# Two key units between the value tiles instead of ahead of them

## The chip, the cores and the metric

One core of a Trainium2 chip runs the whole program. The metric is the device time of one execution in microseconds (us), as the median of several runs. A profiled execution gives, beside its own time, the span from the first to the last instruction and the trace of every engine: TensorE (PE in the rows; PEld is its weight load), VectorE (DVE), ScalarE (ACT), GpSimd (POOL) and SyncE's queue of transfers (SPq). Every engine works through a queue of its own in the order in which the program gives it.

## What is computed

A decoder trunk of two layers over 1024 positions of width 1024. Only the first layer's mixer is touched: a native sparse attention beside a short gated convolution, both fed by one input projection.

```python
def even_mixer(h, w_in, cmp_pe, cmp_w1, cmp_w2, conv_w, w_out, cos, sin):
    z = h @ w_in
    q = apply_rope(z[..., :o1]...)                    # 8 heads of 64
    kv = z[..., o1:o2].reshape(bsz, s, 6, A_KV_HEADS, HEAD_DIM)
    gates = z[..., o2:o3]
    bc = z[..., o3:]                                  # short convolution
    kc = compress(apply_rope(kv[:, :, 0], cos, sin), cmp_pe[0], cmp_w1[0], cmp_w2[0])
    vc = compress(kv[:, :, 1], cmp_pe[1], cmp_w1[1], cmp_w2[1])
    ks = apply_rope(kv[:, :, 2], cos, sin)            # keys of the selected blocks
    kw = apply_rope(kv[:, :, 4], cos, sin)            # keys of the window
    o_a = nsa_attention(q, kc, vc, ks, kv[:, :, 3], kw, kv[:, :, 5], gates)
    ...
```

After it come the output projection, a gated convolution FFN, a recurrent layer and a second FFN; none of them is changed.

## The kernel before

Activations lie with features on the partitions and positions on the free axis. All products are made at near full precision from two halves: every operand is split into a rounded part (`wh`, `hh`) by a copy on ACT and a remainder (`wl`, `hl`) by a subtraction on DVE, and `mm3` (L144 to L148) issues three matmuls for each product, one of them with `wl` and one with `hl`.

The projection's columns come in pieces:

- A **unit** (`units`, L163) is 128 features by 1024 positions: 48 matmuls of 512 columns into one tile `U` of PSUM. The generator `gen` gives eight of them in the order compress keys, compress values, selected keys, window keys, four query units. The first two run together; `load_w` brings the weights of each later one (a 512 KB transfer into `wr`, then `wh` on ACT L132 and `wl` on DVE L133). `wr`, `wh` and `wl` have two buffers each.
- `c_unit` (L521) turns a compress unit into `xc`: rotation (`rope_unit`, for the keys), four copies into the staging tile `xf` on ACT (L532), and the split into `xc` (L151 on ACT, L152 on DVE). There is one `xf`: the second unit's copies wait until DVE has read the first one's.
- `k_unit` (L510) turns a key unit into `KH` and `KL`: four copies of 32 partitions on ACT (`rz`, L503 and L504), three full passes on DVE (`rz`, `rt`, L505 to L507), two copies to `KH` (L517) and two subtractions to `KL` (L518). It puts four duplicating copies on the list `dups`; they are issued on ACT after the value stage (L1034, L1035).
- A **value tile** (`v_proj`, L651) is 128 positions by 280 columns (four value heads' columns and 24 gates): 24 matmuls of 280 columns into a tile `V` of the same four PSUM buffers as `U`, then one copy on ACT and two operations on DVE (`VS` L667 and L668, `GS` L669). There are eight. Their weights `wvh`, `wvl` come in three pieces of 3, 3 and 2 chunks (`v_weights`, L640). After five tiles, and again after all eight, `cmp_mm` (L592) makes the compress hidden layer: 48 matmuls of 132 columns into `ub`, with two weight loads of 512 KB.

In `even_layer` the order written is: two compress units, key unit 0, weights of the value tiles, key unit 1, eight value tiles with the two `cmp_mm`, the duplicating copies, the query units. A scheduler places the instructions of each engine in a queue; it follows the written order, and may bring a later instruction forward where it takes an earlier one to be waiting. Once built, the queues are fixed.

Of the kernel before, what the change touches and what calls it, by code (L numbers as in the profile page):

```python
# [59 lines left out]
class Kern:  # L60
# [590 lines left out]
    def v_proj(self, H, wh, wl):  # L651
        nc, io = self.nc, self.io
        w1 = self.cmp_w(0)
        hvs = []
        for tt in range(8):
            if tt == self.vsplit:
                hvs.append(self.cmp_mm(0, w1))
                w1 = self.cmp_w(1)
            U = self.newU("V")
            ts = slice((tt % 4) * P, (tt % 4) * P + P)  # L660
            for kc in range(KC):
                hi, lo = H[kc][tt // 4]
                self.mm3(U[:, :280], hi[:, ts], lo[:, ts], wh[:, kc], wl[:, kc], kc == 0, kc == KC - 1)
            uv = U[:, :256].rearrange("p (b d) -> p b d", b=4)
            rc = self.rcol[:, tt:tt + 1]
            hi = self.VS[tt][:, :, :64]
            nc.scalar.activation(hi, uv, AF.Copy, scale=rc)  # L667
            nc.vector.scalar_tensor_tensor(self.VS[tt][:, :, 64:], uv, rc, hi.bitcast(FP), op0=OP.mult, op1=OP.subtract)  # L668
            nc.vector.tensor_scalar(self.GS[:, tt], U[:, 256:280], rc, None, op0=OP.mult)  # L669
        hvs.append(self.cmp_mm(1, w1))  # L670
        nc.scalar.activation(self.GS, self.GS, AF.Sigmoid)
        return hvs

    def select(self, i, imp):
        nc, tp = self.nc, self.tp
# [280 lines left out]
    def even_layer(self, fin):  # L956
# [9 lines left out]
        def opened(name, **kw):  # L966
            st = ExitStack()
            return st, st.enter_context(self.pool(name, **kw))
# [16 lines left out]
        H = nm["H"]  # L985
# [4 lines left out]
        with self.pool("xp", side="right") as xp, self.pool("np0", side="right") as self.np:  # L990
# [26 lines left out]
            gen = self.units(srcs, H, 2, mid, ws, 4)  # L1017
            U0 = next(gen)
        with self.pool("xc", side="right") as xc:
            self.XC = [[xc.tile([P, 2, 8, 68], FR, name=f"xc{a}{b}") for b in range(2)] for a in range(2)]  # L1020
            with self.pool("xf", side="right") as xf:
                self.xf = xf.tile([P, 2, 8, 68], FP, name="xf")
                nc.vector.memset(self.xf[:, :, :, 64:], 0.0)
                self.c_unit(0, U0)
                self.c_unit(1, next(gen))
            vs, vp = opened("VS")
            self.VS = [vp.tile([P, 4, P], FR, name=f"VS{t}") for t in range(8)]
            with self.pool("wv") as wp:
                Us, self.dups = [next(gen)], []
                wv = self.v_weights(wp)  # L1030
                self.k_unit(0, Us[0])
                self.k_unit(1, next(gen))
                hvs = self.v_proj(H, *wv)
            for o, t in self.dups:  # L1034
                nc.scalar.activation(o, t, AF.Copy)  # L1035
            box = self.compress1(cp, hvs)
# [734 lines left out]
```

## Time and profile before

| | |
|---|---|
| median of 3 runs | 2360.34 us (2357.21 to 2365.05) |
| profiled execution, own time | 2362.92 us |
| its span, first to last instruction | 2361.0 us |
| PE busy in the span | 2271.9 us (96%) |
| DVE, ACT, POOL busy | 1672.5 us (71%), 1162.0 us (49%), 137.3 us (6%) |

The shares are means over stages that have different limits. The change lies between about 37 and 104 us of the span, so the rows further down are read from there: which engine has a gap, and which instruction of which other engine ended last before the gap closed. A row of the timeline has the start and the length in us, the engine, the line, the operation, what it writes and reads, how many instructions the row merges and, in brackets, how long the engine stood idle before it and what ended that.

### The profile page before, as it was taken

The numbers are of one execution on the slowest core, as the hardware profiler recorded it, in microseconds if no ns is written. First come the engines' busy times: TensorE is split into PE (matmuls) and PEld (weight loads), VectorE is DVE, ScalarE is ACT, GpSimd is POOL, SyncE is SP. The second block draws the span as 40 slices with busy tenths as digits, with TensorE's granted clock in tenths as the row PEclk, the third lists the DMA queues.
The fourth block names the chain that finished last, engine by engine and source line by source line (L and its number), as shares of the span: only waits on it lengthen the run. The fifth ranks groups of instructions, "written<-read, shape, count | busy, mean of one in ns | idle before, by whom it ended". The sixth has DMA issues, their size and how long they took to land.

```text
span 2361.0 us, 26600 instructions
## 1 busy us (share of the span) xinstructions
PE 2271.9 (96%) x10190; PEld 1830.7 (78%) x10190; DVE 1672.5 (71%) x2459; ACT 1162.0 (49%) x1718; POOL 137.3 (6%) x102
## 2 busy tenths in 40 slices
PE   8999998999989999999999999999899999999998
PEld 6877776777667888887888777887678888878876
DVE  5566878988798777777434766768987777773446
ACT  7653666666645444444111474575554444441114
POOL 0002233311000000000000300000000000000000
PEclk9999999999999999999999999999999999999999
DMA  4223112222512222216222101113122222162222
GB/s 145 77 74 107 42 54 83 79 81 86 205 52 76 84 84 84 84 65 232 99 78 74 59 30 63 45 47 116 54 90 81 81 81 81 63 242 88 81 77 76
DMA packets 70464, 206.24 MB, mean 87 GB/s; under 512 B 7873, under 2 KB 11457, under 8 KB 70209
## 3 DMA queue, kind: packets, MB, share of 16 engines
q1 hardware_dynamic: 65376, 194.83, 24.1%
q10 hardware_dynamic: 4320, 7.61, 0.9%
q8 instruction: 80, 1.31, 0.2%
q0 software_dynamic: 640, 2.10, 0.2%
q14 instruction: 48, 0.39, 0.1%
HBM read 162.57 MB, written 41.94 MB: 87 GB/s over the span
## 4 chain that ended last, share of the span: by engine, by line
PE 72%; DVE 10%; ACT 5%; issue 2%; DMA 1%; POOL 0%; DVEq 0%; ACTq 0%; POOLq 0%
PE q L146 11%; PE q L148 11%; PE q L147 11%; PE D L148 7%; PE D L146 7%; PE D L147 7%; PE U L147 2%; PE U L146 2%; PE U L148 2%; PE T L842 2%; PE O L825 2%; PE F L146 1%; PE F L147 1%; PE F L148 1%; DVE P L817 1%
## 5 line engine op out<-in xcount | busy, mean ns | idle before, releaser
L132 ACT ACTIVATE wh<-wr 128x1024 fp32r<-128x1024 f32 x112 | 118.5, 1059 | 375.2 <-PE D L147 282.9
L1250 ACT ACTIVATE z<-q 128x512 f32<-128x512 f32 x176 | 103.7, 593 | 363.0 <-PE q L148 358.0
L264 DVE TENSOR_TENSOR x<-D,x 128x512 f32<-128x512 f32 x192 | 124.1, 686 | 216.2 <-PE D L148 216.1
L258 DVE SCALAR_TENSOR_TENSOR o<-z,par,o 128x1023 f32<-128x1023 f32 (+1 forms) x176 | 225.6, 1282 | 27.9 <-ACT o L256 24.9
L146 PE MATMUL q<-h,sh 128*128 128x512 f32 x480 | 190.3, 396 | 3.6 <-ACT z L1250 3.6
L148 PE MATMUL q<-h,sl 128*128 128x512 f32 x480 | 189.2, 394 | 0.0
L147 PE MATMUL q<-h,sh 128*128 128x512 f32 x480 | 188.7, 393 | 0.0
L146 PE MATMUL D<-y,wh 128*128 128x512 f32 (+1 forms) x464 | 181.1, 392 | 0.3 <-ACT y L151 0.3
L148 PE MATMUL D<-y,wl 128*128 128x512 f32 (+1 forms) x464 | 180.8, 390 | 0.0
L147 PE MATMUL D<-y,wh 128*128 128x512 f32 (+1 forms) x464 | 180.8, 390 | 0.0
L146 PE MATMUL U<-hh,wh 128*128 128x512 f32 x400 | 159.5, 399 | 12.1 <-ACT wh L132 12.1
L147 PE MATMUL U<-hl,wh 128*128 128x512 f32 x400 | 158.9, 398 | 0.0
L148 PE MATMUL U<-hh,wl 128*128 128x512 f32 x400 | 158.4, 397 | 0.0
L146 PE MATMUL q<-h,wh 128*128 128x512 f32 x320 | 126.5, 395 | 4.1 <-ACT wh L151 4.1
L133 DVE TENSOR_TENSOR wl<-wr,wh 128x1024 fp32r<-128x1024 f32 x88 | 111.5, 1266 | 26.6 <-ACT wh L132 23.3
L148 PE MATMUL q<-h,wl 128*128 128x512 f32 x320 | 127.6, 399 | 0.6 <-DVE wl L152 0.5
L147 PE MATMUL q<-h,wh 128*128 128x512 f32 x320 | 126.9, 397 | 0.0
L802 ACT ACTIVATE P<-P,m 128x640 f32<-128x640 f32 (+7 forms) x128 | 93.5, 731 | 46.9 <-DVE m L800 46.4
L256 ACT ACTIVATE o<-z,par 128x1024 f32<-128x1024 f32 x88 | 108.6, 1234 | 7.1 <-DMA fd<-o 4.5
L152 DVE TENSOR_TENSOR pl<-T,ph 128x512 fp32r<-128x512 f32 x132 | 89.3, 686 | 30.9 <-ACT ph L151 27.9
L1253 DVE TENSOR_TENSOR z<-q,z 128x512 f32<-128x512 f32 x132 | 90.1, 687 | 28.7 <-PE q L148 28.7
L146 PEld LDWEIGHTS q<-h,sh 128*128 128x128 f32 x480 | 90.4, 188 | 25.5 <-ACT z L1250 4.5
(362 smaller groups left out, 5777.8 us busy)
## 6 DMA issues: line engine op xcount, KB each, us to landing
wv<-in_wup SPq DMA_DIRECT2D x44, 512.0 KB, 5.4
wr<-in_wup SPq DMA_DIRECT2D x44, 512.0 KB, 4.7
fd<-o SPq DMA_DIRECT2D x44, 512.0 KB, 3.0
wr<-in_wd SPq DMA_DIRECT2D x40, 512.0 KB, 3.7
yr<-fd SPq DMA_DIRECT2D x36, 512.0 KB, 4.3
wr<-in_wbc SPq DMA_DIRECT2D x24, 512.0 KB, 3.5
wr<-in_cin SPq DMA_DIRECT2D x16, 512.0 KB, 3.6
yd<-y SPq DMA_DIRECT2D x24, 256.0 KB, 2.0
```

Of the source, the lines that this page charges most:

```text
L132: nc.scalar.activation(hi[:, s], raw[:, s], AF.Copy)
L133: eng.tensor_tensor(lo[:, s], raw[:, s], hi[:, s].bitcast(FP), op=OP.subtract)
L146: mm(out, whi, xhi, start=first, stop=False, skip_group_check=resumed)
L147: mm(out, whi, xlo, start=False, stop=False, skip_group_check=resumed)
L148: mm(out, wlo, xhi, start=False, stop=last, skip_group_check=resumed)
L152: (eng or self.nc.vector).tensor_tensor(lo, t, hi.bitcast(FP), op=OP.subtract)
L256: nc.scalar.activation(o, src, AF.Identity, bias=b, scale=w(K - 1))
L258: nc.vector.scalar_tensor_tensor(o[:, s:], src[:, :n - s], w(K - 1 - s), o[:, s:], op0=OP.mult, op1=OP.add)
L264: nc.vector.tensor_tensor(x, ps, x, op=OP.add)
L802: nc.scalar.activation(p, p, AF.Exp, bias=m, scale=-1.0, accum_out=s)
L1250: self.nc.scalar.activation(out, x, AF.Copy)
L1253: self.nc.vector.tensor_tensor(out, a, b, op=op)
```

## The change

`v_proj` becomes a generator that stops after each value tile and gives the compress results last. `even_layer` loads the value weights first, then makes three value tiles, key unit 0, three value tiles, key unit 1, and the last two.

```diff
--- before.py
+++ after.py
@@ -667,9 +667,10 @@
             nc.scalar.activation(hi, uv, AF.Copy, scale=rc)
             nc.vector.scalar_tensor_tensor(self.VS[tt][:, :, 64:], uv, rc, hi.bitcast(FP), op0=OP.mult, op1=OP.subtract)
             nc.vector.tensor_scalar(self.GS[:, tt], U[:, 256:280], rc, None, op0=OP.mult)
+            yield None
         hvs.append(self.cmp_mm(1, w1))
         nc.scalar.activation(self.GS, self.GS, AF.Sigmoid)
-        return hvs
+        yield hvs
@@ -1025,12 +1026,18 @@
             self.VS = [vp.tile([P, 4, P], FR, name=f"VS{t}") for t in range(8)]
-            with self.pool("wv") as wp:
-                Us, self.dups = [next(gen)], []
-                wv = self.v_weights(wp)
-                self.k_unit(0, Us[0])
-                self.k_unit(1, next(gen))
-                hvs = self.v_proj(H, *wv)
+            wst, wp = opened("wv")
+            wv = self.v_weights(wp)
+            self.dups = []
+            vgen = self.v_proj(H, *wv)
+            for br, tt in ((0, 3), (1, 3)):
+                for _ in range(tt):
+                    next(vgen)
+                self.k_unit(br, next(gen))
+            hvs = []
+            for hv in vgen:
+                hvs = hv
+            wst.close()
             for o, t in self.dups:
                 nc.scalar.activation(o, t, AF.Copy)
```

The number of instructions on each engine stays the same, and from the first query unit on the queues of before and after are equal. Up to there they differ. Three places follow; the number behind a tile's name tells tiles of one kind apart.

TensorE where the first two (compress) units end, before: `U_297` is the second compress unit, `U_474` key unit 0.

```order
L147 MATMUL U_297<-hl_290,wh_206 128x512
L148 MATMUL U_297<-hh_289,wl_207 128x512
L146 MATMUL U_474<-hh_185,wh_392 128x512
L147 MATMUL U_474<-hl_186,wh_392 128x512
L148 MATMUL U_474<-hh_185,wl_393 128x512
```

The same place after: `V_500`, `V_528` and `V_556` are the first three value tiles, `U_584` is key unit 0, with the same weights `wh_392`.

```order
L147 MATMUL U_297<-hl_290,wh_206 128x512
L148 MATMUL U_297<-hh_289,wl_207 128x512
L146 MATMUL V_500<-wvh,hh_185 128x280
L146 MATMUL V_528<-wvh,hh_185 128x280
L146 MATMUL V_556<-wvh,hh_185 128x280
L146 MATMUL U_584<-hh_185,wh_392 128x512
L147 MATMUL V_500<-wvl,hh_185 128x280
```

The value tiles' first matmuls, which need `wvh`, now stand directly behind the compress units; one matmul of key unit 0 is between them, the other 47 stand behind the three tiles.

ScalarE at the same place, before: `rz_543` belongs to key unit 0, `xf` and `xc` to the compress units, `wvh` are the value weights.

```order
L132 ACTIVATE wh_525<-wr_523 128x1024
L532 ACTIVATE xf<-rt_411 64x8x64 x4
L151 ACTIVATE xc_401<-xf 128x1088
L503 ACTIVATE rz_543<-U_474 32x1024
L504 ACTIVATE rz_543<-U_474 32x1024
L532 ACTIVATE xf<-rt_450 64x8x64 x4
L503 ACTIVATE rz_543<-U_474 32x1024
L151 ACTIVATE xc_403<-xf 128x1088
L504 ACTIVATE rz_543<-U_474 32x1024
L151 ACTIVATE wvh<-wr_531 128x840
```

After:

```order
L532 ACTIVATE xf<-rt_411 64x8x64 x4
L151 ACTIVATE xc_401<-xf 128x1088
L532 ACTIVATE xf<-rt_450 64x8x64 x4
L151 ACTIVATE xc_403<-xf 128x1088
L151 ACTIVATE wvh<-wr_476 128x840
L151 ACTIVATE wvh<-wr_480 128x840
L151 ACTIVATE wvh<-wr_484 128x560
```

The weights of key unit 1 and the copies of key unit 0 are gone from this stretch; `wvh` still stands behind both compress units' `xf` and `xc`.

ScalarE ahead of the first query unit, before: `wh_1027` are that unit's weights, `VS` and `GS` the value tiles' results.

```order
L667 ACTIVATE VS_469<-V_859,rcol 128x4x64
L667 ACTIVATE VS_470<-V_887,rcol 128x4x64
L671 ACT_TABLE_LOAD
L671 ACTIVATE GS<-GS 128x192
L132 ACTIVATE wh_1027<-wr_1025 128x1024
```

After, from the weights of the second `cmp_mm` on (`wh_765`); `U_797` is key unit 1.

```order
L132 ACTIVATE wh_765<-wr_763 128x1024
L503 ACTIVATE rz_846<-U_797 32x1024
L504 ACTIVATE rz_846<-U_797 32x1024
L503 ACTIVATE rz_846<-U_797 32x1024
L504 ACTIVATE rz_846<-U_797 32x1024
L667 ACTIVATE VS_469<-V_859,rcol 128x4x64
L667 ACTIVATE VS_470<-V_887,rcol 128x4x64
L517 ACTIVATE KH_126<-rt_847 64x1024
L517 ACTIVATE KH_127<-rt_847 64x1024
L672 ACT_TABLE_LOAD
L672 ACTIVATE GS<-GS 128x192
```

and directly behind these:

```order
L1042 ACTIVATE KH_126<-rt_847 64x1024
L1042 ACTIVATE KL_130<-KL_130 64x1024
L1042 ACTIVATE KH_127<-rt_847 64x1024
L1042 ACTIVATE KL_131<-KL_131 64x1024
L132 ACTIVATE wh_1027<-wr_1025 128x1024
```

The whole work on key unit 1, its four duplicating copies included, now stands between the second `cmp_mm`'s weights and those of the first query unit.

## Rows read from the trace of the kernel before

**Rows 1.** Windows: length; busy us (instructions) of PE, PEld, DVE, ACT, POOL; PEclk; DMA.

```profile
37.50:60.00 22.50, 22.50 (x97) 17.89 (x95) 9.09 (x9) 18.61 (x19) 0.00 (x0) 1.00 0.10 34
60.00:84.30 24.30, 19.38 (x123) 18.90 (x123) 19.11 (x24) 22.31 (x25) 0.00 (x0) 0.86 0.30 99
84.30:104.20 19.90, 19.90 (x169) 19.90 (x169) 6.84 (x14) 8.72 (x13) 0.00 (x0) 1.00 0.18 54
104.20:160.00 55.80, 55.32 (x241) 44.60 (x240) 30.39 (x36) 32.85 (x40) 0.00 (x0) 1.00 0.20 59
```

**Rows 2.** Timeline of PE, key units, value tiles and both compress products.

```profile
53.38 0.39 PE L148 MATMUL U<-hh,wl 128*128 128x512 f32 x1
...
59.69 0.39 PE L148 MATMUL U<-hh,wl 128*128 128x512 f32 x1
60.79 0.40 PE L146 MATMUL V<-wvh,hh 128*128 128x280 f32 x1 [0.71 <-ACT wvh L151]
62.21 0.50 PE L147 MATMUL V<-wvl,hh 128*128 128x280 f32 x1 [1.03 <-DVE wvl L152]
...
79.43 0.57 PE L146 MATMUL V<-wvh,hh 128*128 128x280 f32 x1 [3.18 <-DVE GS L669]
...
84.13 0.23 PE L146 MATMUL ub<-xc,wh 128*128 128x132 f32 x1
...
89.44 0.34 PE L146 MATMUL V<-wvh,hh 128*128 128x280 f32 x1
...
98.75 0.23 PE L146 MATMUL ub<-xc,wh 128*128 128x132 f32 x1
...
104.06 0.44 PE L146 MATMUL U<-hh,wh 128*128 128x512 f32 x1
```

**Rows 3.** Timeline of ACT, from the second compress unit's copies to the value weights.

```profile
52.21 4.37 ACT L532 ACTIVATE xf<-rt 64x512 f32<-64x512 f32 x4
...
57.65 1.11 ACT L151 ACTIVATE xc<-xf 128x1088 fp32r<-128x1088 f32 x1
...
59.83 1.70 ACT L151 ACTIVATE wvh<-wr 128x840 fp32r<-128x840 f32 x2
...
65.09 0.67 ACT L151 ACTIVATE wvh<-wr 128x560 fp32r<-128x560 f32 x1 [1.50 <-DMA wr<-in_wv]
```

**Rows 4.** Timeline of DVE and the transfer queue in the same stretch.

```profile
50.27 1.29 DVE L152 TENSOR_TENSOR xc<-xf,xc 128x1088 fp32r<-128x1088 f32 x1 [4.50 <-ACT xc L151]
...
61.13 1.97 DVE L152 TENSOR_TENSOR wvl<-wr,wvh 128x840 fp32r<-128x840 f32 x2
...
62.18 0.33 SPq L647 DMA_DIRECT2D wr<-in_wv  x1
...
65.80 0.74 DVE L152 TENSOR_TENSOR wvl<-wr,wvh 128x560 fp32r<-128x560 f32 x1 [0.30 <-ACT wvh L151]
```

**Rows 5.** Groups, 35 to 130 us: count | busy us, mean ns | idle before, releaser.

```profile
L133 DVE TENSOR_TENSOR wl<-wr,wh 128x1024 fp32r<-128x1024 f32 x10 | 12.2, 1224 | 15.7 <-ACT wh L132 15.7
L132 ACT ACTIVATE wh<-wr 128x1024 fp32r<-128x1024 f32 x9 | 9.4, 1058 | 13.8 <-PE U L147 8.0 <-PE ub L147 5.7
L504 ACT ACTIVATE rz<-U 32x1024 f32<-32x1024 f32 x9 | 9.2, 1019 | 0.1
L505 DVE TENSOR_TENSOR rt<-U,rope 128x1024 f32<-128x1024 f32 x4 | 4.9, 1223 | 5.5 <-ACT rz L504 5.5
L1035 ACT ACTIVATE KH<-rt 64x1024 fp32r<-64x1024 f32 x4 | 4.2, 1056 | 0.1
L517 ACT ACTIVATE KH<-rt 64x1024 fp32r<-64x1024 f32 x4 | 4.2, 1053 | 0.1
L668 DVE SCALAR_TENSOR_TENSOR VS<-V,rcol,VS 128x256 fp32r<-128x256 f32 x8 | 3.8, 481 | 8.9 <-ACT VS L667 8.8
L671 ACT ACT_TABLE_LOAD x1 | 1.3, 1283 | 0.0
L671 ACT ACTIVATE GS<-GS 128x192 f32<-128x192 f32 x1 | 0.4, 364 | 0.0
```

## Prediction, made before the changed kernel ran

> **What bounds the kernel now.** I read the busy shares first, then the windows of the stretch that the change touches, then TensorE's timeline there, then the other engines' timelines backwards from the instruction for which TensorE waits. From the first query unit on TensorE is all but full (55.32 of 55.80 us) at the full clock, and the queues there are not changed [rows 1]. So the question is one number: by how much does the start of the first query unit (104.06 us [rows 2]) move?
>
> TensorE's stream from the end of the compress units to that start has these parts. A key unit: nine steps of three matmuls take 59.69 - 53.38 = 6.31 us, 0.70 us each, 0.234 us a matmul; a unit has 16 steps, 11.2 us [rows 2]. Two of them end with the last matmul at 59.69 plus 0.23, at 59.92 us, so the first began at 59.92 - 22.44 = 37.5 us. A value tile: three take 98.75 - 89.44 = 9.31 us, 3.10 us each, 0.129 us a matmul. A compress product `ub`: 89.44 - 84.13 = 5.31 us, and 104.06 - 98.75 gives the same [rows 2]. Together 22.44 + 8 x 3.10 + 2 x 5.31 = 57.9 us of work, in 104.06 - 37.5 = 66.6 us. **8.7 us are lost**: 0.9 us between 59.92 and the first value matmul at 60.79; 1.3 us for `wvl`; 3.2 us at 79.43, where a value tile waits for a PSUM buffer that DVE frees late, being busy with key work [rows 2]; and about 3.3 us at half clock, because PEclk is 0.86 over the 24.30 us that hold these waits: 1.2 GHz for 0.28 of them, 6.8 us, costs half of that [rows 1]. That is the most the change could give back.
>
> The reader should also see what the key units do for others. While TensorE runs them (37.5 to 60 us) ACT is busy 18.61 of 22.5 us [rows 1]: this is where `xf` and `xc` of the compress units are made, and `wvh` stands behind them in ACT's queue and starts at 59.83 [rows 3]. The key units are the cover of that work.
>
> **The change part by part.** The instructions stay the same, their durations too. I follow TensorE's new queue, using the rows' durations.
>
> *Step 1, the first value matmul.* It stands directly behind the compress units and needs `wvh`. The new ACT queue ahead of `wvh` loses the key unit's copies and one weight split, but keeps both `xf` and both `xc`. The first `xf` and `xc` run as before; DVE reads `xf` from 50.27 for 1.29 us, to 51.56 [rows 4], and only then may the second `xf` be written. Then 4.37 us of `xf` and 1.11 us of `xc` [rows 3]: `wvh` starts at 57.1 us, only 2.7 us earlier than before. TensorE started 60.79 - 59.83 = 0.96 us after `wvh` began [rows 2, 3], hence at 58.1. It is free at 37.5: **20.6 us of waiting** where 0.9 was. Key unit 0 has its operands, but 47 of its 48 matmuls stand behind the three value tiles.
>
> *Step 2, the rest of the weights.* DVE makes the low part of `xc` (1.29 us) from 57.1 to 58.4, then `wvl`; TensorE followed 62.21 - 61.13 = 1.08 us after its start [rows 2, 4], so at 59.5. The third piece can be fetched when `wvl` has released its buffer, at 59.5 too: in the trace 65.09 - 62.18 = 2.9 us to `wvh`, then 0.67 and 0.74 us [rows 3, 4], so it is ready at 63.8. Until then TensorE has the matmuls of the first pieces: 17 at half clock (the wait at 62.21 was followed by such a stretch; two stretches share the 6.8 us, so 3.4 us each, a loss of 1.6 to 1.7), plus five more. It goes on at full speed from 63.9 us, having done 25 value matmuls and one of the unit, 3.5 us of the 57.9 us of work.
>
> *Step 3, key unit 1.* 47 value matmuls (6.1 us) and 47 unit matmuls (11.0 us) end at 81.0; two tiles, `ub`, one tile (14.6 us) at 95.6. Key unit 1's weights stand on ACT behind: `wh` for `ub` (1.06, waits for the end of key unit 0), four `rz` (4 x 1.02), then on DVE `rt`, `rz`, one `VS` and `rt` (3 x 1.22 + 0.48), then two `KH` (2 x 1.05), two duplicates (2 x 1.05), then `wh` (1.06) and `wl` (1.22) [rows 5]: 81.0 + 15.7 = 96.7 us. The third matmul of the unit, the first with `wl`, would be due at 96.0. **0.7 us** lost. The unit ends at 96.7 + 46 x 0.234 = 107.5.
>
> *Step 4, the first query unit.* Two tiles and `ub` take TensorE 11.5 us, to 119.0; its third matmul would be due at 119.5. But on ACT from the end of key unit 1: `wh` of `ub` 1.06, four `rz` 4.08, DVE's four operations 4.14, two `KH` 2.11, the table load 1.28, the sigmoid 0.36, four duplicates 4.22, then `wh` 1.06 and `wl` 1.22 of the query unit [rows 5]: 19.5 us, so 127.0. **7.5 us of waiting.** Before, the duplicates lay beside value tiles and this wait did not exist.
>
> *Step 5, the clock.* The trace has no wait as long as 7.5 or 20.6 us in this stretch; the nearest is 3.18 us, followed by half clock [rows 1, 2]. I charge the price of one such stretch, 1.6 us, to the query unit. For the 0.7 us of step 3 the bounds are nothing and 1.6 us; I take nothing, being below the 0.71 and 1.03 us that stood close together at 60 us.
>
> *What goes.* The 3.2 us wait for PSUM goes: a buffer is asked for again four tiles later, which with the units in between is more than 14 us instead of behind key work on DVE.
>
> *The sum.* The query unit's third matmul stood at 104.06 + 2 x 0.23 = 104.5 and now at 127.0: 22.5 us; with step 5, **24 us**. By losses: 20.6 + 0.9 (for `wvl`) + 1.6 + 0.2 + 0.7 + 7.5 + 1.6 = 33 against 8.7. On the profiled execution's own time, 2362.92 us (span 2361.0), that is 2387; it lies 2.6 us above the median of the runs, 2360.34, from which I predict **2384 us**. Behind that point nothing takes it back: TensorE is full there [rows 1], and the other engines wait for its results.
>
> **The rivals.**
>
> *The interleaving works (faster).* DVE's and ACT's key work spreads over the value tiles, no tile waits for PSUM, and the 8.7 us come back: 2352 us. It needs `wvh` ready when TensorE comes to it, at 37.5 us; each us later costs one, and it is a loss from 46 us on. For it speaks the 3.18 us wait [rows 2]; against it ACT's queue, where `xc` of the second compress unit ends at 57.1. Chance 0.02. The Trainium skill (Perfetto Trace Analysis, Optimization Strategy) says that where the most contended engine changes from regime to regime, interleaving the regimes may help. By that rule 2352 would be the forecast; the trace does not agree here, for the key units already run beside another regime, ACT's 18.61 us of compress work [rows 1].
>
> *Only the first wait (slower, less).* ACT gets to the query unit's weights in time, so step 4's 7.5 us and its 1.6 us of clock go: 24 - 9 = 15 us, 2375 us. It would need 7.5 us less in a chain whose parts all stand in one queue. Chance 0.08.
>
> *A dearer clock.* After 20.6 us of idling the half clock lasts twice as long (+1.6) and the 0.7 us wait is followed by one more stretch (+1.6): 27 us, 2387 or 2388 us. Nothing in the rows excludes it. Chance 0.10.
>
> *It is taken back later.* Some later stage waits for something that does not move with TensorE, and the loss shrinks to under 7 us: about 2365 us. The rows show no such work in the 55.80 us behind the stretch [rows 1], and weight transfers are issued as buffers come free. Chance 0.02.
>
> **How the numbers follow.** 0.78 for 2384; the rest as given. The three slower cases hold 0.96, and their times run from 2375 to 2388; with the runs' own scatter (2357.21 to 2365.05) the range is 2374 to 2391. A measurement of this kernel can tell about 0.3%, 7 us: faster by more than that 0.02, within it 0.02, slower 0.96.
>
> **What would show it.** Right: in the profile after, TensorE idle some 20 us up to about 58 us of the span, ended by ACT's `wvh`; a second wait of 6 to 8 us before the first query unit, ended by `wh` or `wl`; that unit's start near 126 us; no wait of a value tile for `GS`. Step 1 is wrong if the first value matmul starts before 50 us, step 4 if the query unit starts within 2 us of the end of `ub`. The forecast as a whole is wrong if the same stretch behind it is shorter than before.

## Result and profile after

| | before | after |
|---|---|---|
| median | 2362.70 us | 2383.15 us (2379.80 to 2385.76) |
| profiled execution, own time | 2362.92 us | 2385.19 us |
| its span | 2361.0 us | 2383.1 us |
| granted clock, mean over the span | 0.987 | 0.982 |

The runs of before were repeated beside those of after, hence a median other than in the table ahead; one of its six runs took 5729 us, the ratio leaves it out, and the other five have a median of 2360.34 us. After takes 1.0085 times as long, 95% interval [1.0072, 1.0098]: 20 us more (17 to 23). The predicted 2384 us and "slower" hold.

The busy times, from the page of after:

```profile
PE 2273.9 (95%) x10190; PEld 1830.2 (77%) x10190; DVE 1667.9 (70%) x2459; ACT 1161.8 (49%) x1718; POOL 137.6 (6%) x102
```

TensorE's busy time has grown by 2.0 us only; the other 20 of the span's 22.1 us are idle time.

The windows of after, with the columns of [rows 1]; the first three are the windows of before, the last two hold what came between them and the full stretch:

```profile
37.50:60.00 22.50, 2.81 (x9) 2.29 (x10) 9.38 (x10) 14.07 (x14) 0.00 (x0) 0.57 0.02 6
60.00:84.30 24.30, 24.30 (x146) 22.00 (x146) 4.91 (x9) 7.45 (x10) 0.00 (x0) 0.98 0.27 83
84.30:104.20 19.90, 19.49 (x127) 17.42 (x126) 10.44 (x16) 12.35 (x15) 0.00 (x0) 1.00 0.21 69
104.20:130.00 25.80, 19.33 (x120) 17.18 (x119) 10.96 (x14) 17.80 (x20) 0.00 (x0) 0.80 0.18 59
130.00:185.00 55.00, 54.51 (x238) 43.90 (x237) 30.72 (x35) 31.81 (x40) 0.00 (x0) 1.00 0.14 42
```

From 37.5 to 60 us TensorE was busy for 22.50 us before and is for 2.81 us now. From 60 to 84.3 us it gained: 24.30 of 24.30 us where it had 19.38. The second loss is in the window up to 130 us, at a mean clock of 0.80. From 130 us on the stream is as full as before from 104 us on.

What TensorE waited for between 35 and 145 us (engine, line, waited for: us, times, longest):

```profile
PE V L146 <- ACT wvh L151: 20.0, 1, 20.0
PE U L146 <- ACT wh L132: 6.4, 1, 6.4
PE U L148 <- DVE wl L133: 0.4, 1, 0.4
PE V L147 <- DVE wvl L152: 0.2, 1, 0.2
```

The wait of 3.18 us for `GS` [rows 2] is gone. The same waits in TensorE's timeline, the two long ones beside the matmul before them:

```profile
36.64 0.40 PE L148 MATMUL U<-hh,wl 128*128 128x512 f32 x1
57.02 1.07 PE L146 MATMUL V<-wvh,hh 128*128 128x280 f32 x3 [19.98 <-ACT wvh L151]
...
58.68 0.60 PE L147 MATMUL V<-wvl,hh 128*128 128x280 f32 x1 [0.17 <-DVE wvl L152]
...
95.65 0.50 PE L148 MATMUL U<-hh,wl 128*128 128x512 f32 x1 [0.41 <-DVE wl L133]
...
117.87 0.27 PE L148 MATMUL ub<-xc,wl 128*128 128x132 f32 x1
124.57 0.80 PE L146 MATMUL U<-hh,wh 128*128 128x512 f32 x1 [6.43 <-ACT wh L132]
...
125.83 0.80 PE L148 MATMUL U<-hh,wl 128*128 128x512 f32 x1
```

ACT's timeline after shows why, in two places: the first answers to [rows 3], the second is the run of work ahead of the first query unit's weights.

```profile
50.77 4.26 ACT L532 ACTIVATE xf<-rt 64x512 f32<-64x512 f32 x4 [1.36 <-DVE xc L152]
55.06 1.11 ACT L151 ACTIVATE xc<-xf 128x1088 fp32r<-128x1088 f32 x1
56.08 1.68 ACT L151 ACTIVATE wvh<-wr 128x840 fp32r<-128x840 f32 x2
61.36 0.67 ACT L151 ACTIVATE wvh<-wr 128x560 fp32r<-128x560 f32 x1 [3.59 <-DMA wr<-in_wv]
...
106.46 1.06 ACT L132 ACTIVATE wh<-wr 128x1024 fp32r<-128x1024 f32 x1 [6.62 <-PE U L147]
...
115.60 2.14 ACT L517 ACTIVATE KH<-rt 64x1024 fp32r<-64x1024 f32 x2 [2.26 <-DVE rt L507]
117.76 1.28 ACT L672 ACT_TABLE_LOAD   x1
119.06 0.36 ACT L672 ACTIVATE GS<-GS 128x192 f32<-128x192 f32 x1
119.43 1.05 ACT L1042 ACTIVATE KH<-rt 64x1024 fp32r<-64x1024 f32 x1
...
122.40 1.04 ACT L1042 ACTIVATE KL<-KL 64x1024 fp32r<-64x1024 f32 x1
123.46 2.00 ACT L132 ACTIVATE wh<-wr 128x1024 fp32r<-128x1024 f32 x2
```

By 37.04 us TensorE has both compress units behind it, and key unit 0's operands are there (DVE ends their low part at 35.2 us). It stands until 57.02 us, because `wvh` starts on ACT at 56.08 us, directly behind the second `xc`. The second wait ends when ACT reaches `wh` at 123.46 us, after the table load, the sigmoid and four duplicating copies.

**Where the loss ends up.** As one mark of the work behind the stretch I take the first copies of `Q` (ACT, L546 and in experiments the same line): 124.1 us before, 147.1 after, 23.0 us later. The first matmul of `D` on `y` much further on moves from 1184.0 to 1206.6, by 22.6; the span by 22.1. Nothing behind the stretch gives much back. The mark is used below because it lies close behind the stretch: a whole run also holds what scatters further on. In e3 below, for one, the profiled execution took 2358.55 us, 4.4 less than that of before, though its `Q` comes 1.8 us later.

### The profile page after: what moved, and what is told of

The parts are those of the page before. It is cut to its first block, busy times and chain, and to the rows that moved or that the text cites. A ratio compares the mean times of both kernels' runs of the same rounds, so it can differ in the third digit from the quotient of the medians.

```text
span 2383.1 us, 26600 instructions
## 1 busy us (share of the span) xinstructions
PE 2273.9 (95%) x10190; PEld 1830.2 (77%) x10190; DVE 1667.9 (70%) x2459; ACT 1161.8 (49%) x1718; POOL 137.6 (6%) x102
## 4 chain that ended last, share of the span: by engine, by line
PE 71%; DVE 10%; ACT 5%; issue 2%; DMA 0%; POOL 0%; DVEq 0%; ACTq 0%; POOLq 0%
PE q L146 11%; PE q L148 11%; PE q L147 11%; PE D L148 7%; PE D L146 7%; PE D L147 7%; PE U L146 2%; PE U L147 2%; PE U L148 2%; PE T L843 2%; PE O L826 2%; PE F L146 1%; PE F L147 1%; PE F L148 1%; DVE P L818 1%
## 5 line engine op out<-in xcount | busy, mean ns | idle before, releaser
L146 PE MATMUL q<-h,wh 128*128 128x512 f32 x320 | 126.5, 395 | 4.0 <-ACT wh L151 4.0
```

The lines of the kernel that those rows point to most:

```text
L146: mm(out, whi, xhi, start=first, stop=False, skip_group_check=resumed)
```

## Experiments

All kernels are the changed one with the edit shown, except e6. "Q" is the start of the first `Q` copy in the trace, in brackets the shift against before (124.1 us); the ratio is against before, with its interval. Each kernel has one trace, and the traces differ ahead of the changed stretch already: the instruction that makes `R` (ACT, L232), which no edit touches, starts between 32.58 and 33.54 us. "Net" is the shift of Q counted from that instruction; differences of less than 1 us in "Q" alone mean nothing.

| run | median us | ratio to before | Q | net | TensorE's waits, 35 to 120 us |
|---|---|---|---|---|---|
| after | 2383.15 | 1.0085 [1.0072, 1.0098] | 147.1 (+23.0) | +23.6 | 20.0, 6.4, 0.4, 0.2 |
| e1 | 2366.34 | 1.0022 [1.0014, 1.0031] | 129.4 (+5.3) | +5.6 | 11.8 |
| e2 | 2381.58 | 1.0080 [1.0067, 1.0093] | 143.8 (+19.7) | +20.0 | 20.0, 2.3, 0.4, 0.2 |
| e3 | 2365.48 | 1.0007 [0.9998, 1.0015] | 126.0 (+1.8) | +2.8 | 6.4, 1.2, 0.3 |
| e4 | 2361.01 | 0.9991 [0.9982, 0.9999] | 121.8 (-2.3) | -1.4 | 2.3, 1.2, 0.5, 0.3 |
| e5 | 2367.50 | 1.0021 [1.0011, 1.0030] | 130.5 (+6.3) | +6.3 | 4.7, 1.4, 0.5 |
| e7 | 2362.99 | 0.9996 [0.9987, 1.0005] | 127.0 (+2.8) | +3.2 | 2.9, 1.4, 1.2, 0.5, 0.3 |
| e8 | 2363.35 | 0.9999 [0.9989, 1.0009] | 126.5 (+2.4) | +3.3 | 4.5, 2.9 |
| e6 | 2355.73 | 0.9968 [0.9957, 0.9980] | 119.0 (-5.1) | -4.9 | 2.1 |

### One unit back to its old place (e1)

```diff
             wst, wp = opened("wv")
+            Us, self.dups = [next(gen)], []
             wv = self.v_weights(wp)
-            self.dups = []
+            self.k_unit(0, Us[0])
             vgen = self.v_proj(H, *wv)
-            for br, tt in ((0, 3), (1, 3)):
+            for br, tt in ((1, 3),):
```

> One half of the change undone: key unit 0 is written ahead of the value weights again; then three value tiles, key unit 1, five tiles. Theory (two waits at the head of a queue): key unit 0 covers TensorE for 11.2 us, so the wait for the value weights falls from 20 to 9 to 11 us, and behind key unit 1 there are now 26 us of tiles and compress products for a chain of 19.5 us, so the wait for the first query unit's weights is gone. Losses about 11 + 0.9 + 1.6 (half clock) = 13.5 us against 8.7 before: 5 us slower than before, 18 faster than the change. Rival (interleaving slows the value tiles themselves): a wait of about 10 us less, but the rest of the loss stays: 13 us slower than before.

The only wait of TensorE up to 120 us, in the list of waits and in the timeline of e1:

```profile
PE V L146 <- ACT wvh L151: 11.8, 1, 11.8
60.28 1.07 PE L146 MATMUL V<-wvh,hh 128*128 128x280 f32 x3 [11.75 <-ACT wvh L151]
```

With 11.2 us of key work back ahead of the value tiles the first wait is 8.2 us shorter, at 11.8 us somewhat above the 9 to 11 expected: not by the whole unit, since `wvh` starts at 59.32 us instead of 56.08, with work of the unit ahead of it on ACT. So the unit is cover and competitor at once, and more the former. The second wait is gone too: behind key unit 1 now stand five value tiles and both compress products, which cover its copies and duplicates. Of 23.0 us 5.3 remain.

### The duplicating copies out of the way (e2)

```diff
-            for o, t in self.dups:
-                nc.scalar.activation(o, t, AF.Copy)
             box = self.compress1(cp, hvs)
@@ the loop over the query units
             U = next(gen)
+            if hh == 0:
+                for o, t in self.dups:
+                    nc.scalar.activation(o, t, AF.Copy)
```

> The change, with the duplicating copies issued behind the first query unit instead of ahead of it. Theory: they are 4.2 of the 19.5 us in the chain from key unit 1 to the first query unit's weights, so the wait of 6.4 us there falls to 2.2 us; 4.2 us faster than the change, 5.8 if TensorE's clock then stays up; the wait of 20 us does not move. Rival (the waiting only moves: the copies have to run at some time, and TensorE waits for them at the next weights): as slow as the change, within 1 us.

The two long waits of e2:

```profile
PE V L146 <- ACT wvh L151: 20.0, 1, 20.0
PE U L146 <- ACT wh L132: 2.3, 1, 2.3
```

Four copies of 1.05 us moved behind `wh`: the second wait falls from 6.4 to 2.3 us, by what they take, and Q comes 3.3 us earlier, net 3.6. The half clock behind the shorter wait is longer, 5.9 instead of 4.8 us, which takes 0.6 us back. In the run times the gain is not clear of the noise: 1.0080 lies inside the interval of after. What remains of the wait are the table load, the sigmoid and `wh` itself.

### The value weights ahead of the compress units' work (e3, e4)

```diff
             U0 = next(gen)
+        wst, wp = opened("wv", side="right")
+        wv = self.v_weights(wp)
         with self.pool("xc", side="right") as xc:
@@ in the value stage
-            wst, wp = opened("wv")
-            wv = self.v_weights(wp)
```

The pool of the weights lives on another side of the memory, and closes later (that line is left out here); nothing of the order between units and tiles is changed. e4 has this and the edit of e2.

> The change, with the value weights written ahead of the compress units' rotation and splits (and their tiles placed elsewhere in SBUF), so that ACT splits them before its work on xf and xc. Theory: TensorE finds the first piece when it gets to it, and waits 1 to 3 us for the third piece's transfer instead of 20 us; the query unit's wait of 6.4 us and its half clock stay. 19 to 21 us faster than the change, so within 4 us of before. Rival (the interleaving slows the value tiles themselves, by contention or PSUM): the wait of 20 us turns into many smaller ones, and half of the loss or more stays, 10 us or more slower than before.

> Both edits of the last two runs: value weights first, duplicating copies behind the first query unit. Theory: the two effects add, since they stand at the two ends of the stretch: 4 to 6 us faster than the run with the weights alone, so 1 to 4 us faster than before. Rival (only one of the two waits counts, the other would be made up later): the same time as with the weights alone.

ACT's timeline in e3: the first `wvh` and the second compress unit's `xc`.

```profile
34.79 0.90 ACT L151 ACTIVATE wvh<-wr 128x840 fp32r<-128x840 f32 x1
...
56.21 1.11 ACT L151 ACTIVATE xc<-xf 128x1088 fp32r<-128x1088 f32 x1
```

`wvh` is made 21 us earlier, ahead of `xf` and `xc` instead of behind them. The wait of 20.0 us is gone, and 21.1 of the 23.0 us of Q with it (+23.0 to +1.8); the second wait stays at 6.4 us. With both edits (e4) both are small, and Q gains net 25.0 us, against 20.8 + 3.6 = 24.4 for the two alone: the waits add up, neither moved into the other. Without them the interleaved order is at 0.9991 of before: the whole loss lay in two places of ACT's queue, where the operands of TensorE's next work stood behind other work.

### Other splits (e5, e7): two misses

Both are e4 with key unit 0 after one tile (e5) or two (e7), and the first compress product earlier.

```diff
-        self.vsplit = 5
+        self.vsplit = 3
@@ in the value stage; e7 has 4 and ((0, 2), (1, 3))
-            for br, tt in ((0, 3), (1, 3)):
+            for br, tt in ((0, 1), (1, 3)):
```

> As the run with both edits, and the key units placed earlier: one value tile, key unit 0, three tiles (the first compress product after the third tile instead of the fifth), key unit 1, four tiles. Theory: behind key unit 1 TensorE now has four tiles and a compress product, 17.7 us, for a chain of 15.3 us on ACT and DVE, so the last wait of 2.3 us goes and its half clock with it; what is left of the 8.7 us lost before is about 1.5 us for the third weight piece: the first query unit starts 6 to 8 us earlier than before. Rival (the chain only moves: key unit 1's weights come later relative to TensorE, which then waits in front of key unit 1): at most as fast as the run with both edits, 2 us earlier than before.

> As the run with both edits, with two value tiles, key unit 0, three tiles (first compress product after the fourth tile), key unit 1, three tiles. Theory: behind key unit 1 there are 14.6 us of TensorE work for a chain of 15.3 us, so about 1 us of waiting and, if the clock falls, 1.6 us more; the same in front of key unit 1 (14.6 us for 15.7). The first query unit starts 4 to 7 us earlier than before. Rival (the place of the key units does not matter once the weights are early): the same as the run with both edits, 2 us earlier.

Both came out later than e4, by 8.6 and 5.1 us of Q (net 7.7 and 4.5), not earlier. In e7 key unit 1 now waits 1.4 us for its `wh`, the query unit 2.9 us instead of 2.3, and there are two stretches at half clock, of 3.4 and 4.8 us, instead of one of 3.4: 2.0 us more of waiting and 2.4 us of clock. In e5 the cause is of another kind, shown by ACT, by the windows of its compress product and what follows, and by TensorE's timeline:

```profile
52.94 4.39 ACT L532 ACTIVATE xf<-rt 64x512 f32<-64x512 f32 x4 [1.36 <-DVE xc L152]
...
58.32 1.09 ACT L151 ACTIVATE xc<-xf 128x1088 fp32r<-128x1088 f32 x1
...
61.49 0.47 ACT L667 ACTIVATE VS<-V,rcol 128x256 fp32r<-128x256 f32 x1
...
62.00:64.00 2.00, 1.22 (x6) 1.25 (x7) 0.63 (x2) 1.99 (x2) 0.00 (x0) 0.58 0.24 94
64.00:76.00 12.00, 12.00 (x57) 12.00 (x57) 8.31 (x11) 8.81 (x11) 0.00 (x0) 0.50 0.13 44
76.00:78.00 2.00, 2.00 (x15) 1.93 (x15) 1.23 (x1) 1.97 (x4) 0.00 (x0) 1.00 0.00 0
...
62.78 0.45 PE L146 MATMUL ub<-xc,wh 128*128 128x132 f32 x1 [4.67 <-DVE GS L669]
63.03 0.42 PE L147 MATMUL ub<-xc,wh 128*128 128x132 f32 x1
63.24 0.42 PE L148 MATMUL ub<-xc,wl 128*128 128x132 f32 x1
```

`ub` takes one of the four PSUM buffers, and the value tile before it in that buffer is read out only when ACT comes to its `VS` at 61.49 us: behind the second `xf`, a weight split, `xc` and two copies of key unit 0, which in e4 come behind the first `VS`. It is the wait of before for `GS` again [rows 2], and the expectation had left it out. It ends after 4.67 us at 62.78, and then TensorE runs at a granted clock of 0.50, 1.2 GHz, until 76.0 us, although it is busy all the time. The matmuls of `ub` follow each other every 0.21 us; at full clock it is 0.11. Over 13.2 us that costs 6.6 us, and the waits are 2.3 us longer than in e4 (6.6 against 4.3 us); a second stretch of 3.4 us at half clock both have. Together 8.9 us, for a net shift of 7.7: the account is about 1 us too high, and e4 loses about 1 us more than its list of waits says (62.8 us from its first value matmul to the query unit for 57.9 us of work, with waits of 3.8).

### What stands behind the wait (e8)

The same wait, but with a value tile and not `ub` behind it: e5 with four tiles ahead of `ub`.

```diff
-        self.vsplit = 3
+        self.vsplit = 4
-            for br, tt in ((0, 1), (1, 3)):
+            for br, tt in ((0, 1), (1, 4)):
```

> As e5_one_then_three, with four value tiles instead of three in the first piece (tile, key unit, three tiles, U for the first query unit's upper half, and so on), so that the tile behind the waiting matmuls has 280 columns, and the 132-column matmuls come only after a tile that doesn't wait. Theory 'what follows the wait decides': the TensorE wait of some 3 to 5 us stays, but the half-clock stretch behind it is 3 to 4 us as after the other waits, not 13; the first query unit's copies of Q start 4 to 6 us earlier than in e5 (at 124.5 to 126.5 instead of 130.5), and the median is 2361 to 2364. Rival 'the place or the wait itself decides': the half clock lasts 10 us or more again, Q at 129 to 131, median 2366 to 2368.

Windows and timeline of e8 at that place:

```profile
59.00:61.00 2.00, 0.00 (x0) 0.00 (x0) 0.88 (x2) 1.95 (x4) 0.00 (x0) 0.81 0.58 170
61.00:63.00 2.00, 1.28 (x5) 1.31 (x6) 0.57 (x2) 1.96 (x3) 0.00 (x0) 0.50 0.24 92
63.00:67.00 4.00, 4.00 (x19) 4.00 (x19) 4.00 (x6) 0.84 (x2) 0.00 (x0) 0.50 0.00 0
67.00:68.00 1.00, 1.00 (x10) 1.00 (x10) 0.59 (x4) 0.51 (x2) 0.00 (x0) 0.96 0.00 0
...
61.72 0.57 PE L146 MATMUL V<-wvh,hh 128*128 128x280 f32 x1 [4.48 <-DVE GS L669]
```

The wait is nearly the same, 4.48 us and for `GS`; the half clock ends at 67.1 us, 5.4 us after the restart instead of 13.2. 7.8 us less of half clock are worth 3.9 us, the waits are 0.8 us longer, and Q comes net 3.1 us earlier than in e5; the median falls to 2363.35 us. That goes with the theory, though the stretch is longer than the 3 to 4 us I gave it. One point stays open: in e8 the clock fell some 1.5 us ahead of the restart (the window 59 to 61 us has 0.81), in e5 some 0.5 us (62 to 64 us has 0.58), so the moment at which it fell differs too. Nor does `ub` take the clock away by itself: before, it ran at a granted 1.00 behind value tiles (84.30 to 104.20 us in [rows 1]), and in e5 the clock came back 2.9 us after a value tile had followed it. That long half clock hangs on what follows the wait is what this pair suggests; it isn't settled by it.

### The old order with early weights (e6)

The kernel before, with the edit of e3 and nothing else:

```diff
+        wst, wp = opened("wv", side="right")
+        wv = self.v_weights(wp)
         with self.pool("xc", side="right") as xc:
@@ in the value stage
-            with self.pool("wv") as wp:
-                Us, self.dups = [next(gen)], []
-                wv = self.v_weights(wp)
-                self.k_unit(0, Us[0])
-                self.k_unit(1, next(gen))
-                hvs = self.v_proj(H, *wv)
+            self.dups = []
+            self.k_unit(0, next(gen))
+            self.k_unit(1, next(gen))
+            hvs = self.v_proj(H, *wv)
```

> The kernel before, its order of units and tiles kept, with the value weights written ahead of the compress units' splits. Theory: TensorE no longer waits 0.7 and 1.0 us for them and keeps its clock (1.6 us), so the first query unit starts about 4 us earlier; the wait of 3.2 us for a PSUM buffer that DVE frees late stays, since both key units' work still meets the tiles at once. Rival (the waits for the weights stand in for others behind them): the tiles get to the PSUM wait earlier and wait longer there, so the query unit starts less than 1 us earlier.

The list of waits has one line for this stretch:

```profile
PE V L146 <- DVE rt L505: 2.1, 1, 2.1
```

The 0.71 and 1.03 us for the value weights [rows 2] and the half clock behind them are gone, the wait for PSUM is 2.1 instead of 3.18 us, where the expectation let it stay at 3.2. With 3.4 us of half clock, worth 1.7, it leaves 3.8 of the 8.7 us lost before, 4.9 less; Q comes net 4.9 us earlier. The median is 2355.73 us, 0.9968 [0.9957, 0.9980] of before: faster than both kernels, and faster than the same weights with the interleaved order (e3, 1.0007 [0.9998, 1.0015], or e4, with the duplicating copies moved too, 0.9991 [0.9982, 0.9999]). The gain over before lies at the edge of what a measurement of this kernel tells from no change, but the interval excludes it.

## Why the prediction held, step by step

The trace of after begins 0.63 us earlier than that of before (`R` on ACT starts at 32.91 instead of 33.54 us), so 0.63 is added to its times where they stand beside predicted ones.

| step | predicted | measured |
|---|---|---|
| 1: first wait of TensorE | 20.6 us, first tile at 58.1 | 20.0 us, at 57.02 + 0.63 = 57.7 |
| 2: `wvl`; 26th value matmul | 59.5; 63.9 | 58.68 + 0.63 = 59.3; 62.86 + 0.63 = 63.5 |
| 3: key unit 1, third matmul | 0.7 us lost, at 96.7 | 0.6 us (0.4 of it idle), at 95.65 + 0.63 = 96.3 |
| 4: query unit, third matmul | 7.5 us lost, at 127.0 | 7.4 us, at 125.83 + 0.63 = 126.5 |
| 5: half clock behind it | 1.6 us | 1.8 us |
| `GS` wait | gone | gone |
| sum | 24 us later | 21.9 + 1.8 = 23.7 us later |

The sum is that of the third matmul's shift (126.5 - 104.6) and step 5. Less the 0.63 us it is the 23.0 of Q, to 0.1 us. On the profiled executions' own times the shift is 22.3 us, by the ratio 20 (17 to 23). The predicted 24 us lie just above that interval; that 2384 comes within 1 us of the measured median is in part luck, for it was counted from 2360.34 us, and later medians of before are 2362.04 to 2363.41 us.

**Step 1** held by its mechanism, which e1 and e3 show from two sides: put the cover back or make the weights earlier, and the wait goes. Its size came from ACT's rows alone: the second `xf`, `xc`, then `wvh`, and that is the order and the length seen after.

**Step 2** was 0.4 us too late. I let TensorE go on with the 26th value matmul at 63.9 us; it starts at 63.5. The third piece was fetched and split as predicted (its `wvh` at 61.36 + 0.63 = 62.0 us, predicted 62.4), so TensorE came to it only as it was ready, and the list of waits has none for it. The clock was back at 61.1 + 0.63 = 61.7 us. One sum of this step is off, without effect on the time, which the third piece sets: 17 matmuls at half clock, 0.234 us each, take 4.0 us by that spacing and not 3.4. The 0.4 us stay to the end of key unit 0 (80.6 us, predicted 81.0) and so to step 3, whose chain from there is 15.7 us long as predicted.

**Step 3** and **step 4** held within 0.6 us. e2 shows the duplicates' share of step 4: 4.2 of it.

**Step 5** took the price of one half-clock stretch of before, 3.4 us at half speed. The windows of after behind the first and the second wait:

```profile
57.00:61.00 4.00, 3.81 (x14) 3.29 (x15) 2.48 (x3) 0.76 (x1) 0.00 (x0) 0.50 0.29 77
61.00:62.00 1.00, 1.00 (x9) 0.97 (x8) 0.00 (x0) 0.64 (x1) 0.00 (x0) 0.96 0.80 197
...
124.00:128.00 4.00, 3.39 (x7) 2.29 (x8) 2.72 (x4) 3.42 (x5) 0.00 (x0) 0.50 0.29 81
128.00:130.00 2.00, 2.00 (x7) 1.55 (x7) 0.00 (x0) 0.00 (x0) 0.00 (x0) 0.66 0.86 326
```

A mean of 0.66 over the last 2 us is 1.36 us at 0.50, so the clock is back at 129.4: 4.8 us behind the restart at 124.57, and 3.5 us behind the third matmul, whose half is the 1.8 us of the table. Behind the first wait it is 4.1 us, to 61.1, where step 2 took 3.4.

**The rivals.** *Interleaving works* fell in the form in which the kernel was run: `wvh` was ready at 57 us, not by 46. In e3 and e4 the weights are early enough, and there the order gives nothing (1.0007) and 2 us (0.9991: 0 to 4) instead of 8.7; e6 gets 7.6 (5 to 10) with the old one. *Only the first wait* fell: the second one is there at 6.4 us, and stays when the first is taken away (e3). *A dearer clock* fell in its two parts: 20.0 us of idling were followed by 4.1 us at half clock and not by twice 3.4; the 0.4 us wait by none (the window up to 104.2 us is at 1.00). *Taken back later* fell for the greater part: of 23.0 us at the first query unit, 22.1 reach the end in the profiled execution; in the medians it is 17 to 23.

Not explained is a small rest: in e7 and e8 the shift of Q (+2.8, +2.4) lies 1.6 and 0.3 us above the interval of the ratio; in the other seven it lies inside. Each shift is that of one execution, the ratio that of many.

## What to carry to other kernels

Before work is put elsewhere, ask what its present place covers: read from the other engines' queues when the operands of the work that comes to the head will be ready, and count the work ahead of it as one sum in queue order. Two units of 11 us each were the cover of the 20 us until ACT had come to `wvh`; with the weights made ahead of that work the same interleaving was level with before. It is worth trying that remedy without the new order too: the old order with early weights was the fastest of all.

## What was unexpected of the hardware

The time at half clock after a wait does not follow from the length of the wait. Counted in each trace, from the restart (or from where the clock fell, if that came later) to the return of the granted clock to 1.00:

| idle before, us | at half clock, us |
|---|---|
| 20.0 | 4.1 (after), 4.5 (e2) |
| 11.8 | 4.9 (e1) |
| 6.4 | 4.8 (after), 4.7 (e3) |
| 4.7 and 4.5 | 13.2 (e5), 5.4 (e8) |
| 3.2 | 3.4 (before) |
| 2.9 | 4.8 (e7), 3.4 (e8) |
| 2.3 | 5.9 (e2) |
| 2.3, then 0.5 | 3.4 (e4) |
| 2.1 | 3.4 (e6) |
| 1.4, then 0.5 | 3.4 (e5), 3.4 (e7) |
| 0.7, then 1.0 | 3.4 (before) |

The same wait of 2.3 us, for the same `wh`, was thus followed by 5.9 us in e2, more than the 20.0 us were, and by 3.4 in e4. The windows show one difference, the moment at which the clock fell. In e2 it fell at 119.9 us, ahead of the restart at 120.77; in e4 TensorE restarted at 99.34 us at full clock, and it fell only at 101.0, behind another 0.5 us of waiting. First e2, then e4:

```profile
119.00:121.00 2.00, 0.23 (x1) 0.23 (x2) 0.77 (x2) 1.96 (x4) 0.00 (x0) 0.72 0.00 0
121.00:125.00 4.00, 3.96 (x9) 2.67 (x10) 1.04 (x2) 3.96 (x5) 0.00 (x0) 0.50 0.38 131
125.00:127.00 2.00, 2.00 (x6) 1.58 (x6) 1.14 (x1) 1.98 (x2) 0.00 (x0) 0.57 0.00 0
...
100.00:102.00 2.00, 1.47 (x5) 1.16 (x5) 0.62 (x2) 1.99 (x3) 0.00 (x0) 0.74 0.27 39
102.00:104.00 2.00, 2.00 (x6) 1.51 (x6) 0.00 (x0) 1.98 (x3) 0.00 (x0) 0.50 0.57 223
104.00:106.00 2.00, 2.00 (x10) 1.59 (x9) 1.23 (x1) 1.97 (x3) 0.00 (x0) 0.90 0.00 0
```

So what a wait costs in clock was not to be read from its length alone, and a difference of 1.3 us between two kernels, half of 5.9 - 3.4, can be this. The stretch of e5 is the odd one: from 64 to 76 us TensorE was busy for 12.00 of 12.00 us, and the clock stayed at 0.50.
